# Copying the sample's and the cross units' probabilities by DMA into fp32r tiles before they are transposed

## The chip, the cores and the metric

The kernel runs on one core of one Trainium2 chip. The metric is the device time of one execution in microseconds; a time given for a kernel is the median of several runs, and a profile is one further execution with the hardware profiler on. Five engines work in parallel, each through its own list in order: TensorE (PE; its weight loads are shown apart as PEld), VectorE (DVE), ScalarE (ACT), GpSimd (POOL) and SyncE (SP), which here only issues DMAs. ACT's queue issues DMAs too.

## The reference

One layer of an encoder for two inputs with the same weights, a prompt of 1024 tokens and a sample of 512, both with 1024 channels and 256 memory tokens. Cut to what matters:

```python
h = rms_norm(x, ln_pre)
z = h @ w_in                      # q, k, v, gates, cross queries, merge logits
pool_out  = multiscale_pool(pool_in, w_pool, pool_scale)
attn_out  = softmax(q @ k.T * scale) @ v            # 8 heads of 64, 2 kv heads
cross_out = softmax(xq @ mk.T * scale) @ mv         # 4 heads of 128, 256 memory tokens
merged = sum(sigmoid(merge_n) * ((branch_n * silu(gate_n)) @ w_branch[n]) for n in range(3))
y = x + rms_norm(merged @ w_out, ln_post)
```

All of it is in float32. The kernel multiplies in fp32r, a reading of float32 that PE takes at a higher rate; each operand is split into a high and a low part (`split`: ACT copies into an fp32r tile, DVE subtracts), and three or two products of the parts are added up.

## The kernel before

Weights come in tiles of 128x1024 (`raw`), are split into `whi` and `wlo`, and are used once. First all projections of the prompt are made, then those of the sample. The softmax work is cut into **units**, which `stream` (line 918) walks through as a pipeline. There are 64 attention units of the prompt (128 queries, 1024 keys), 8 cross units of the prompt, 16 pair units of the sample's attention (`pairs_of`, two blocks of 128 queries by 512 keys), and 4 cross units of the sample (`cross`, 512 queries by 256 memory tokens, one head each), in that order. The text calls the last four c0 to c3.

Step i of `stream` calls, for several units at once: `ahead` two units early (loads), `scores` of unit i (matmuls into a PSUM tile `A`, then row maximum on DVE, exponentials on ACT into an SBUF tile `u`, reciprocal on DVE, normalization on POOL in place), `turn` of unit i-3 (eight transposes of 128x128 on PE into another `A`, then `split` into a `med` tile), `values` of unit i-6 (matmuls with v), and `hand` of unit i-1. `weave` fills the rest of PE's time from another stream of work: the sample's projections and, near the end of the units, the first merge phase of `branches` (matmuls written B<-med,whi and B<-med,wlo).

The normalized probabilities are plain f32, since POOL writes them. For the 64 attention units, `hand` (line 810) copies them by a DMA on ACT's queue (line 814) into a second `u` tile of type fp32r, and `turn` transposes that with the identity `identr`. The pair and the cross units have no `hand` (None in their tuples): `turn` transposes the f32 tile with `ident`, and the tile is held until then.

There are 7 buffers for `u`, 14 for `med`, 9 for `hu`, 3 for `A`, 2 for `B`. The order on each engine is not the order of the code: a scheduler sets it when the program is built, by priorities (`tc.high_priority`) and by its own idea of durations, and it also decides which buffer a tile takes. So a change of one operation moves others.

Of the kernel before, what the change touches and what calls it, by code (L numbers as in the profile page):

```python
# [12 lines left out]
F32 = mybir.dt.float32  # L13
F32R = mybir.dt.float32r
# [5 lines left out]
P = 128  # L20
D = 1024
KC = D // P
BLK = 512
TT = BLK // P
NH, NG, HD = 8, 2, 64
NXH, XHD, NMEM = 4, 128, 256
# [36 lines left out]
def encoder_kernel(ctx: ExitStack, tc, wt, xs, xts, mt, cols, rows, rope, edge, ys):  # L63
    nc = tc.nc
    v, act, pool, pe = nc.vector, nc.scalar, nc.gpsimd, nc.tensor
# [10 lines left out]
    def nm(s):  # L76
        count[0] += 1
        return f"{s}_{count[0]}"

    def U(dt=F32, n=D):  # L80
        return sb.tile([P, D + 2 * PAD], dt, tag="u", bufs=NU, name=nm("u"))[:, :n]

    def M(dt=F32R):
        return sb.tile([P, 2048], dt, tag="med", bufs=NM, name=nm("med"))
# [7 lines left out]
    def A(dt=F32):  # L92
        return ps.tile([P, 1024], dt, tag="A", bufs=3, name=nm("A"))
# [32 lines left out]
    def mm(out, l, r, **k):  # L126
        cost[0] += out.free_size() / 2.4
        pe.matmul(out, l, r, **k)  # L128

    def tr(out, x, i):  # L130
        cost[0] += 107 if i is ident else 56
        pe.transpose(out, x, i[:])  # L132
# [7 lines left out]
    def load(out, src):  # L140
        return nc.sync.dma_start(out, src)  # L141
# [3 lines left out]
    ident = const.tile([P, P], F32, name="ident")  # L145
    make_identity(nc, ident)
    identr = const.tile([P, P], F32R, name="identr")
# [15 lines left out]
    def lo_of(out, x, hi):  # L163
        v.tensor_tensor(out, x, hi.bitcast(F32), op=ALU.subtract)  # L164

    def split(hi, lo, x):
        act.activation(hi, x, AF.Copy)  # L167
        lo_of(lo, x, hi)
# [599 lines left out]
    def from_scratch(field, bs, dt=F32):  # L768
# [3 lines left out]
            load(t[:, c * BLK:(c + 1) * BLK], field[c][:, bs])  # L772
        return t

    def attention(b, sc, kt, vt):

        bs = slice(b * BLK, (b + 1) * BLK)
        qd, gd, out = sc["q"], sc["attn_gate"], sc["br1"]
        nch = KC
        units = [(jp, hd, j) for jp in range(TT // 2) for hd in range(NH) for j in range(2)]  # L780
        state = {}

        def ahead(i):
            jp, hd, j = units[i]
            for k, x in ((3, 0), (1, 1)):
                if i == 0 or (i + k) % (2 * NH) == 0 and i + k < len(units):
                    at = 0 if i == 0 else jp + 1
                    if x == 0:
                        state["q", at] = M()
                    load(state["q", at][:, x * D:(x + 1) * D].bitcast(F32), qd[b * TT + at * 2 + x][:])  # L790

        def scores(i):
            jp, hd, j = units[i]
            g = hd // (NH // NG)
            q = state["q", jp][:, j * D + hd * P:j * D + (hd + 1) * P]
            a = A()
            for n in range(2):
                ns = slice(n * 512, n * 512 + 512)
                mm(a[:, ns], q, kt[g][0][:, ns], start=True, stop=False)
                mm(a[:, ns], q, kt[g][1][:, ns], start=False, stop=True)  # L800
            mx, sm, rc = S(1), S(1), S(1)
            with tc.high_priority(PMAX):
                v.reduce_max(mx[:], a[:], axis=AX.X, negate=True)  # L803
                p = U()
                act.activation(p, a[:], AF.Exp, bias=mx[:], accum_out=sm[:])  # L805
            v.reciprocal(rc[:], sm[:])  # L806
            pool.tensor_scalar(p, p, rc[:], 1.0, op0=ALU.mult, op1=ALU.mult)  # L807
            state[i] = p

        def hand(i):  # L810

            p = state[i]
            state[i] = U(F32R)
            act.dma_start(state[i].bitcast(F32), p)

        def turn(i):
            jp, hd, j = units[i]
            p = state.pop(i)
            if j == 0:
                state["pt", i // 2] = M()[:], M()[:]  # L820
            pv = [t.rearrange("p (c j n) -> p c j n", c=nch, j=2) for t in state["pt", i // 2]]
            tp = A(F32R)
            for c in range(nch):
                tr(tp[:, c * P:(c + 1) * P], p[:, c * P:(c + 1) * P], identr)
            tv = tp[:].bitcast(F32).rearrange("p (c n) -> p c n", c=nch)
            with tc.high_priority(PTURN):
                split(pv[0][:, :, j], pv[1][:, :, j], tv)

        def values(i):

            jp, hd, j = units[i]
            g = hd // (NH // NG)
            if j == 0:
                state["o"] = B()
            o, pts = state["o"], state["pt", i // 2]
            for c in range(j * nch // 2, (j + 1) * nch // 2):
                for s in range(2):
                    mm(o[:, :256], vt[:, c, g].rearrange("p s d -> p (s d)"), pts[s][:, c * 256:(c + 1) * 256],
                       start=(c == 0 and s == 0), stop=(c == nch - 1 and s == 1))
            if j == 0:  # L840
                return
            del state["pt", i // 2]
            gated(state, jp, hd, o, gd, out, b)

        return [(ahead, scores, turn, values, hand, i, 2560) for i in range(len(units))]

    def pairs_of(sc, kt, vt):

        qd, gd, out = sc["q"], sc["attn_gate"], sc["br1"]
        units = [(jp, hd) for jp in range(TT // 2) for hd in range(NH)]  # L850
        state = {}

        def ahead(i):
            jp, hd = units[i]
            for k, x in ((2, 0), (1, 1)):
                if i == 0 or (i + k) % NH == 0 and i + k < len(units):
                    at = 0 if i == 0 else jp + 1
                    if x == 0:
                        state["q", at] = M()
                    load(state["q", at][:, x * D:(x + 1) * D].bitcast(F32), qd[at * 2 + x][:])  # L860

        def scores(i):
            jp, hd = units[i]
            g = hd // (NH // NG)
            a, p = A(), U()
            mx, sm, rc = S(2), S(2), S(2)
            for j in range(2):
                q, ns = state["q", jp][:, j * D + hd * P:j * D + (hd + 1) * P], slice(j * BLK, (j + 1) * BLK)
                mm(a[:, ns], q, kt[g][0], start=True, stop=False)
                mm(a[:, ns], q, kt[g][1], start=False, stop=True)  # L870
            with tc.high_priority(PMAX):
                v.reduce_max(mx[:], a[:].rearrange("p (j n) -> p j n", j=2), axis=AX.X, negate=True)
                for j in range(2):
                    ns = slice(j * BLK, (j + 1) * BLK)
                    act.activation(p[:, ns], a[:, ns], AF.Exp, bias=mx[:, j:j + 1], accum_out=sm[:, j:j + 1])
            v.reciprocal(rc[:], sm[:])
            for j in range(2):
                ns = slice(j * BLK, (j + 1) * BLK)
                pool.tensor_scalar(p[:, ns], p[:, ns], rc[:, j:j + 1], 1.0, op0=ALU.mult, op1=ALU.mult)
            state[i] = p  # L880

        def turn(i):
            p, tp, pt = state[i], A(), M()
            for c in range(4):
                for j in range(2):
                    tr(tp[:, c * 256 + j * P:c * 256 + (j + 1) * P], p[:, j * BLK + c * P:j * BLK + (c + 1) * P], ident)
            with tc.high_priority(PTURN):
                split(pt[:, :D], pt[:, D:], tp[:])
            state[i] = pt

        def values(i):
            jp, hd = units[i]
            o, pt = B(), state.pop(i)
            for c in range(4):
                for s in range(2):
                    mm(o[:, :256], vt[:, c, hd // (NH // NG)].rearrange("p s d -> p (s d)"),
                       pt[:, s * D + c * 256:s * D + (c + 1) * 256], start=(c == 0 and s == 0), stop=(c == 3 and s == 1))
            gated(state, jp, hd, o, gd, out, 0)

        return [(ahead, scores, turn, values, None, i, 2560) for i in range(len(units))]  # L900

    def gated(state, jp, hd, o, gd, out, b):
        r = slice((hd % 2) * 64, (hd % 2) * 64 + 64)
# [31 lines left out]
    def cross(b, sc, mkd, mvd, mem):  # L935
# [3 lines left out]
        state = {}  # L939
# [36 lines left out]

        def turn(c):
            p = state[c]
            tp = A()
            for m in range(2):  # L980
                for t in range(TT):
                    tr(tp[:, m * 512 + t * P:m * 512 + (t + 1) * P], p[:, t * 256 + m * P:t * 256 + (m + 1) * P], ident)
            pt = M()
            split(pt[:, 0:1024], pt[:, 1024:2048], tp[:])
            state[c] = pt

        def values(c):
# [8 lines left out]
                v.tensor_tensor(g[:], o[:], g[:], op=ALU.mult)  # L996
            finished.append((out[c][:, bs], g[:]))

        return [(ahead, scores, turn, values, None, c, 3410) for c in range(NXH)]

    def branches(b, sc, merged):

# [171 lines left out]
    units = [u for b in range(2) for u in attention(b, sc, kt, vt)]  # L1174
# [109 lines left out]
```

## Time and profile before

| | us |
|---|---|
| median of 3 runs | 1461.84 (1461.23 to 1462.43) |
| the profiled execution | 1459.46 |
| its span, first to last instruction | 1457.6 |
| PE busy | 1430.3 |
| DVE busy | 966.1 |
| ACT busy | 711.4 |
| POOL busy | 280.3 |

Lines of the form "L132 PE MATMUL A<-identr,u" name the source line, the engine, the operation and the tiles; L128 is the helper for all matmuls, L132 that for all transposes, L141 that for loads, L164 and L167 the two halves of a split. L814 is the copy in `hand`, L803 to L807 the softmax of the attention units, L872 to L879 that of the pair units, L966 to L974 that of the cross units, L996 the gate behind a cross unit's values, L1061 the evacuation of a merge. Something like [2.3 <-DVE med L1061] says how long the engine was idle ahead of the row and what released it. In the windows view each row is a stretch with the busy time of each engine in it.

### The profile page before, as it was taken

The numbers are of one execution on the slowest core, as the hardware profiler recorded it, in microseconds if no ns is written. First come the engines' busy times: TensorE is split into PE (matmuls) and PEld (weight loads), VectorE is DVE, ScalarE is ACT, GpSimd is POOL, SyncE is SP. The second block draws the span as 40 slices with busy tenths as digits, with TensorE's granted clock in tenths as the row PEclk, the third lists the DMA queues.
The fourth block names the chain that finished last, engine by engine and source line by source line (L and its number), as shares of the span: only waits on it lengthen the run. The fifth ranks groups of instructions, "written<-read, shape, count | busy, mean of one in ns | idle before, by whom it ended". The sixth has DMA issues, their size and how long they took to land. (4 is left out here: it accounts for less than half of the span.)

```text
span 1457.6 us, 19545 instructions
## 1 busy us (share of the span) xinstructions
PE 1430.3 (98%) x7264; PEld 1197.1 (82%) x7264; DVE 966.1 (66%) x1211; ACT 711.4 (49%) x1085; POOL 280.3 (19%) x286
## 2 busy tenths in 40 slices
PE   7999999999999999999999999999999999999998
PEld 5878888888888888788888888888888788888887
DVE  6896585766547664665777666686776665665654
ACT  6454444454434544443666666676676223323322
POOL 1000010110000000210223332233342230240241
PEclk9999999999999999999999999999999999999999
DMA  8312243332331444244655665565357834954942
GB/s 292 122 58 95 79 145 104 120 123 68 125 101 62 154 143 133 84 158 163 244 187 193 216 238 192 186 223 184 127 181 244 278 119 157 332 189 157 333 156 82
DMA packets 95375, 238.65 MB, mean 164 GB/s; under 512 B 10672, under 2 KB 18992, under 8 KB 95280
## 3 DMA queue, kind: packets, MB, share of 16 engines
q1 hardware_dynamic: 86064, 203.84, 42.2%
q10 hardware_dynamic: 9216, 33.56, 5.9%
q8 instruction: 57, 0.93, 0.3%
q14 instruction: 38, 0.31, 0.1%
HBM read 151.38 MB, written 52.43 MB: 140 GB/s over the span
## 5 line engine op out<-in xcount | busy, mean ns | idle before, releaser
L128 PE MATMUL B<-med,whi 128*128 128x512 f32 x1576 | 492.4, 393 | 4.5 <-DVE med L1061 2.3
L128 PE MATMUL A<-med,whi 128*128 128x512 f32 x1200 | 373.9, 392 | 1.4 <-ACT med L167 1.0
L128 PEld LDWEIGHTS B<-med,whi 128*128 128x128 f32 x1576 | 291.4, 188 | 64.5 <-DVE med L1061 2.7
L128 PE MATMUL B<-med,wlo 128*128 128x512 f32 x788 | 308.3, 391 | 0.5 <-DVE wlo L164 0.5
L167 ACT ACTIVATE whi<-raw 128x1024 fp32r<-128x1024 f32 (+1 forms) x169 | 167.3, 990 | 283.7 <-PE A L128 147.9
L164 DVE TENSOR_TENSOR wlo<-raw,whi 128x1024 fp32r<-128x1024 f32 (+1 forms) x169 | 210.0, 1243 | 138.1 <-ACT whi L167 137.6
L128 PEld LDWEIGHTS A<-med,whi 128*128 128x128 f32 x1200 | 223.0, 188 | 48.3 <-ACT med L167 1.2
L128 PE MATMUL A<-med,wlo 128*128 128x512 f32 x600 | 234.1, 390 | 0.1
L128 PEld LDWEIGHTS B<-med,wlo 128*128 128x128 f32 x788 | 147.9, 188 | 32.4 <-DVE wlo L164 1.3
L189 POOL TENSOR_SCALAR s<-s 128x16 f32<-128x16 f32 (+3 forms) x17 | 7.5, 444 | 660.9 <-DVE s L582 324.0
L128 PEld LDWEIGHTS A<-med,wlo 128*128 128x128 f32 x600 | 112.6, 188 | 24.7 <-DVE wlo L164 1.0
L164 DVE TENSOR_TENSOR med<-A,med 128x1024 fp32r<-128x1024 f32 (+1 forms) x93 | 112.8, 1214 | 28.4 <-ACT med L167 26.7
L167 ACT ACTIVATE med<-A 128x1024 fp32r<-128x1024 f32 x92 | 94.2, 1025 | 68.8 <-PE A L132 68.4
L807 POOL TENSOR_SCALAR u<-u,s 128x1024 f32<-128x1024 f32 x64 | 72.1, 1126 | 211.8 <-DVE s L806 174.6
L1063 POOL TENSOR_TENSOR med<-med,hu 128x512 f32<-128x512 f32 x48 | 78.7, 1650 | 130.2 <-DVE hu L1061 130.2
L803 DVE TENSOR_REDUCE s<-A 128x1 f32<-128x1024 f32 x64 | 77.8, 1215 | 37.0 <-PE A L128 33.8
L128 PE MATMUL A<-whi,med 128*128 128x512 f32 (+1 forms) x352 | 98.3, 360 | 0.0
L805 ACT ACTIVATE u<-A,s 128x1024 f32<-128x1024 f32 x64 | 71.3, 1114 | 40.6 <-issue 23.4
L128 PE MATMUL A<-kt,med 128*128 128x512 f32 x320 | 87.7, 395 | 0.0
L167 ACT ACTIVATE whi<-sum 128x1024 fp32r<-128x1024 f32 x50 | 52.9, 1061 | 60.3 <-PE B L128 36.5
L164 DVE TENSOR_TENSOR med<-med,med 128x1024 fp32r<-128x1024 f32 (+1 forms) x50 | 55.2, 1115 | 37.8 <-ACT med L167 34.0
L167 ACT ACTIVATE med<-med 128x1024 fp32r<-128x1024 f32 (+1 forms) x44 | 44.3, 1018 | 69.6 <-POOL med L1063 41.7
(199 smaller groups left out, 1915.3 us busy)
## 6 DMA issues: line engine op xcount, KB each, us to landing
raw<-wt SPq DMA_DIRECT2D x168, 512.0 KB, 3.7
u<-u ACTq DMA_DIRECT2D x64, 512.0 KB, 3.2
merge<-hu SPq DMA_DIRECT2D x72, 256.0 KB, 2.2
hu<-merge SPq DMA_DIRECT2D x72, 256.0 KB, 5.3
med<-br SPq DMA_DIRECT2D x36, 256.0 KB, 5.3
q<-hu SPq DMA_DIRECT2D x24, 256.0 KB, 2.5
br<-hu SPq DMA_DIRECT2D x24, 256.0 KB, 2.7
med<-q SPq DMA_DIRECT2D x12, 512.0 KB, 4.8
```

The source lines that it names most:

```text
L128: pe.matmul(out, l, r, **k)
L164: v.tensor_tensor(out, x, hi.bitcast(F32), op=ALU.subtract)
L167: act.activation(hi, x, AF.Copy)
L189: pool.tensor_scalar(ss, ss, EPS, 1.0, op0=ALU.add, op1=ALU.mult)
L803: v.reduce_max(mx[:], a[:], axis=AX.X, negate=True)
L805: act.activation(p, a[:], AF.Exp, bias=mx[:], accum_out=sm[:])
L807: pool.tensor_scalar(p, p, rc[:], 1.0, op0=ALU.mult, op1=ALU.mult)
L1063: pool.tensor_tensor(at, at, sg[:], op=ALU.add)
```

## The change

`hand` moves out of `attention` into a helper `hand_on(state)`, and the pair and cross units pass it too. Their `turn` then reads the fp32r copy, with `identr` and a PSUM tile of type fp32r, whose bits are read as f32 for the split.

```diff
+    def hand_on(state):
+        def hand(i):
+
+            p = state[i]
+            state[i] = U(F32R)
+            act.dma_start(state[i].bitcast(F32), p)
+        return hand
...
-        return [(ahead, scores, turn, values, hand, i, 2560) for i in range(len(units))]
+        return [(ahead, scores, turn, values, hand_on(state), i, 2560) for i in range(len(units))]
...
-            p, tp, pt = state[i], A(), M()
+            p, tp, pt = state[i], A(F32R), M()
...
-                    tr(tp[:, c * 256 + j * P:c * 256 + (j + 1) * P], p[:, j * BLK + c * P:j * BLK + (c + 1) * P], ident)
+                    tr(tp[:, c * 256 + j * P:c * 256 + (j + 1) * P], p[:, j * BLK + c * P:j * BLK + (c + 1) * P], identr)
             with tc.high_priority(PTURN):
-                split(pt[:, :D], pt[:, D:], tp[:])
+                split(pt[:, :D], pt[:, D:], tp[:].bitcast(F32))
...
-        return [(ahead, scores, turn, values, None, i, 2560) for i in range(len(units))]
+        return [(ahead, scores, turn, values, hand_on(state), i, 2560) for i in range(len(units))]
...
-            tp = A()
+            tp = A(F32R)
...
-                    tr(tp[:, m * 512 + t * P:m * 512 + (t + 1) * P], p[:, t * 256 + m * P:t * 256 + (m + 1) * P], ident)
+                    tr(tp[:, m * 512 + t * P:m * 512 + (t + 1) * P], p[:, t * 256 + m * P:t * 256 + (m + 1) * P], identr)
...
-            split(pt[:, 0:1024], pt[:, 1024:2048], tp[:])
+            split(pt[:, 0:1024], pt[:, 1024:2048], tp[:].bitcast(F32))
...
-        return [(ahead, scores, turn, values, None, c, 3410) for c in range(NXH)]
+        return [(ahead, scores, turn, values, hand_on(state), c, 3410) for c in range(NXH)]
```

The orders show two places at the end of the stream. On PE before, the transposes of c1, c2 and c3 (A_10184, A_10253, A_10300) at the point where the first merge matmul (B_10212) begins:

```order
L128 MATMUL B_10125<-med_4471,wlo_10122 128x512
L132 MATMUL A_10184<-ident,u_9988 128x128 x8
L132 MATMUL A_10253<-ident,u_10058 128x128 x8
L132 MATMUL A_10300<-ident,u_10109 128x128 x8
L128 MATMUL B_10212<-med_10196,whi_10208 128x512
L128 MATMUL B_10225<-med_10069,med_4528 128x256 x8
```

The same place in the change, where A_10192 is c0, A_10238 is c1, A_10309 is c2, and B_10266 the first merge matmul:

```order
L132 MATMUL A_10192<-identr,u_10088 128x128 x8
L128 MATMUL B_10177<-med_4468,whi_10173 128x512
L128 MATMUL B_10177<-med_4468,wlo_10174 128x512
L128 MATMUL B_10177<-med_4471,whi_10173 128x512 x2
L128 MATMUL B_10177<-med_4471,wlo_10174 128x512
L128 MATMUL B_10177<-med_4471,whi_10173 128x512 x2
L128 MATMUL B_10177<-med_4471,wlo_10174 128x512
L132 MATMUL A_10238<-identr,u_10142 128x128 x8
L132 MATMUL A_10309<-identr,u_10218 128x128
L128 MATMUL B_10266<-med_10250,whi_10262 128x512
L128 MATMUL B_10279<-med_10119,med_4528 128x256 x5
```

Before, three units were transposed in a row ahead of the merge; now c0 and c1 are, with the first of c2's eight transposes, while the other seven of c2 and all of c3's stand further back among the merge matmuls. Between c3's scores (A_10144, not shown) and c2's first transpose stand 13 matmuls of 512 columns, 8 of values and these 16 transposes.

On ACT in the change, from the copy of c1 to the split of c1 (the copies are of c1, u_10142, and of c2, u_10218; the exponentials are c3's):

```order
L780 DMA u_10142<-u_10036 128x1024
L505 ACTIVATE hu_10233<-B_10177,hbias 128x512
L972 ACTIVATE u_10161,s_10158<-A_10144,s_10157 128x256 x4
L167 ACTIVATE whi_10338<-raw_10336 128x1024
L167 ACTIVATE med_10201<-A_10192 128x1024
L780 DMA u_10218<-u_10108 128x1024
L167 ACTIVATE med_10247<-A_10238 128x1024
```

The copy of c2, on which c2's transposes wait, stands behind c3's exponentials, a split of weights and the split of c0. Before, no DMA stood in this part of ACT's list. Line numbers in the change: the copy is L780, `attention`'s softmax 8 lines lower down than before, and everything from `pairs_of` on 2 lines lower down (L970 becomes L972).

More of the change, by code (lines that the diff above doesn't have):

```diff
@@ L808, in scores @@
             state[i] = p
[L810 to L814, printed above, removed]
         def turn(i):
```

## The prediction

> **What bounds the kernel now.** I read the page first: the busy shares, the slices and the clock.
>
> ```profile
> span 1457.6 us, 19545 instructions
> PE 1430.3 (98%) x7264; PEld 1197.1 (82%) x7264; DVE 966.1 (66%) x1211; ACT 711.4 (49%) x1085; POOL 280.3 (19%) x286
> PEclk9999999999999999999999999999999999999999
> ```
>
> TensorE (PE) is busy for 98% of the span. Matmul ends are modelled, so that share alone proves little; the stretches say where PE has no gap at all. Columns: the stretch in us and its length, busy time of PE, weight loads, DVE, ACT and POOL, then granted clock, DMA share and GB/s. The units that the change touches run from about 978 to 1112.
>
> ```profile
> 978.00:1085.00 107.00, 107.00 (x634) 92.36 (x633) 76.62 (x98) 73.78 (x164) 40.76 (x63) 1.00 0.49 160
> 1085.00:1112.00 27.00, 26.20 (x181) 23.93 (x180) 20.74 (x26) 22.62 (x54) 12.59 (x20) 1.00 0.64 212
> 1144.00:1300.00 156.00, 155.75 (x688) 128.61 (x687) 99.11 (x100) 49.10 (x59) 52.02 (x36) 1.00 0.63 214
> ```
>
> PE is full in the first stretch, short of 0.8 us in the second, and after 1144 short of 0.25 us in 156. So in this kernel PE time is the time: what PE saves before 1112 brings the end forward, and what PE waits there is not given back later. The second stretch is also the one in which ACT is nearly full: 22.62 of 27 us, 84%, against 69% before it. That matters, because the change puts its new work on ACT.
>
> **The transposes, part by part.** 28 units (16 pairs, 12 cross units) with 8 transposes each change from f32 to fp32r, 224 in all. First eight of the kind that is wanted (identr), then eight of the kind that is there (ident), each with what stands behind it on PE; columns are start and duration.
>
> ```profile
> 965.01 0.79 PE L132 MATMUL A<-identr,u 128*128 128x128 f32 x8
> 965.64 1.17 PE L128 MATMUL B<-med,vt 128*128 128x256 f32 x8
> 966.65 1.60 PE L128 MATMUL A<-med,u 128*128 128x256 f32 x12
> 979.75 1.03 PE L132 MATMUL A<-ident,u 128*128 128x128 f32 x8
> 980.54 1.19 PE L128 MATMUL B<-med,vt 128*128 128x256 f32 x8
> 981.57 0.63 PE L128 MATMUL B<-med,whi 128*128 128x512 f32 x2
> 968.32 0.80 PE L132 MATMUL A<-identr,u 128*128 128x128 f32 x8
> 968.95 0.47 PE L128 MATMUL B<-med,whi 128*128 128x512 f32 x1
> 969.25 0.39 PE L128 MATMUL B<-med,wlo 128*128 128x512 f32 x1
> 1022.79 0.39 PE L128 MATMUL B<-med,whi 128*128 128x512 f32 x1
> 1023.09 1.07 PE L132 MATMUL A<-ident,u 128*128 128x128 f32 x8
> 1023.91 0.47 PE L128 MATMUL B<-med,whi 128*128 128x512 f32 x1
> 1024.23 0.40 PE L128 MATMUL B<-med,wlo 128*128 128x512 f32 x1
> ```
>
> From the start of the transposes to the start of the piece after the next: 1.64 us for fp32r (965.01 to 966.65), 1.82 for f32 (979.75 to 981.57): 0.18 less for a unit. Behind a 512-wide matmul the f32 kind costs more: 1022.79 to 1024.23 is 1.44 with the matmul ahead of it, whose own pitch is 0.23, so 1.21, against 0.93 for fp32r (968.32 to 969.25): 0.28 less. In the chain of waits the f32 groups last 0.87 us as a rule, and 0.95 or more in five of the 28, where the dear case is. The first and the last of these five:
>
> ```profile
> 1023.18 0.98 PE A L132 x8
> ...
> 1080.64 0.95 PE A L132 x8
> ```
>
> 23 x 0.18 + 5 x 0.28 = **5.5 us less on PE**. Bounds: 28 x 0.16 (the starts alone, 0.79 against 0.63) = 4.5, and 28 x 0.28 = 7.8.
>
> The Trainium skill speaks of this in "FP8 and Floating Point Precision", section "TensorE Precision Notes": true fp32 makes four passes through the array, the reduced reading one. By that rule the eight f32 transposes would take four times the 0.63 us and the change would save some 53 us, an estimate. The rows above disagree, with 0.79 against 0.63, and the rows decide.
>
> **What is added: 28 copies on ACT's queue.** Each is one issue, with this row, and it moves 512 KB between two tiles:
>
> ```profile
> L814 ACTq DMA_DIRECT2D u<-u x64: 472/472/507, 689.4 to 967.8; - x64
> DMA to landing us min/median/max: 2.9/3.2/6.8
> q10 hardware_dynamic: 9216, 33.56, 5.9%
> PE A L132 <- DMA u<-u: 0.2, 1, 0.2
> ```
>
> An issue holds ACT for 0.47 us, 28 of them 13 us over 134 us: ACT goes from 69% to about 79% in the first stretch, and to 92% in the second if five fall there. The DMA engines: 5.9% of 1457.6 us for 64 copies is 1.34 us each, so 28 add 0.28 of share to 0.49 and 0.64. Both fit; I put the bandwidth at nothing, and at up to 1 us if the weight loads that hide behind PE come late.
>
> In the steady part the latency is covered. By the change's own orders a copy is issued right behind the exponentials of the next unit, and its transposes stand at least 7.8 us of PE work (at the pitches above) behind that unit's scores; the attention units have the same distance, and the last row shows what PE lost to their 64 copies: 0.2 us, once. The pair units need somewhat more of it than attention, since they have two exponentials. I cost them at nothing, at most 2 us. The u tiles: a probability is now held for about one step and its copy for two, one tile of the seven more at a time. The order cannot say what that costs; ACT's exponentials would wait for a buffer, and the same 2 us bounds it. No copy goes through SP's or POOL's queue. ACT's issue waits for POOL's normalization of the unit before, which by the order of ACT is a whole unit old, except at the end.
>
> **The end of the stream** is where the cover is thin. The last four units are the sample's cross units, c0 to c3. Before, PE did the transposes of c1, c2 and c3 in one block of 24 at 1108.42, half a us after the last probability was ready. In the change (the orders shown in the section on the change) the first transpose of c2 stands close behind c3's scores, and c2's copy stands on ACT behind c3's four exponentials, one split of weights and the split of c0. Rows of before for these pieces:
>
> ```profile
> 1099.67 1.59 PE L128 MATMUL A<-med,u 128*128 128x256 f32 x12
> 1103.84 0.47 ACT L970 ACTIVATE u<-A,s 128x256 f32<-128x256 f32 x1 [1.43 <-DVE s L966]
> 1105.65 1.04 ACT L167 ACTIVATE med<-A 128x1024 fp32r<-128x1024 f32 x1
> 1108.39 1.06 ACT L167 ACTIVATE whi<-raw 128x1024 fp32r<-128x1024 f32 x1 [1.30 <-PE B L128]
> L966 DVE TENSOR_REDUCE s<-A 128x4 f32<-128x1024 f32 x9 | 10.9, 1212 | 0.8 <-POOL u L974 0.8
> 1098.89 0.95 PE B L128 x8
> 1101.26 2.75 PE B L128 x12
> 1108.42 2.78 PE L132 MATMUL A<-ident,u 128*128 128x128 f32 x24
> 1112.08 0.50 PE L128 MATMUL B<-med,whi 128*128 128x512 f32 x1 [0.87 <-ACT med L167]
> ```
>
> PE, from the end of c3's scores to c2's first transpose in the new order: 13 matmuls of 512 columns (2.75 / 12 = 0.229 each, 2.98 us), eight values (0.95) and the 16 transposes of c0 and c1 (0.70 for eight): **5.3 us**. ACT, from the same moment: before, c3's scores ended at 1101.26 and its exponentials began at 1103.84, 2.58 us later. Four take 1.81 (1103.84 to 1105.65), then 1.06 for the weights, 1.04 for the split of c0, and 3.2 until the copy lands: **9.7 us**. The difference, **4.4 us**, PE stands still, since it takes its work in order and 12 matmuls of the next phase and everything behind them queue behind that transpose. Bounds: if the exponentials begin as soon as a reduction of 1.21 us allows (1.3 us behind the scores) and the copy lands in 2.9, the wait is 2.8; if the copy takes the longest time seen, 6.8, it is 8.0. I take the middle, since in the new order c0's and c1's scores stand next to each other on PE, so ACT can hardly have less of a backlog than it had at 1103.84. What goes away is the wait of 0.87 us at 1112.08 for ACT's split: by the time the copy has landed that split is done.
>
> A wait of this length also touches the clock. What the profile shows of that is at the kernel's start, a matmul that waited and the three stretches around it (PE alone: length, busy, clock, DMA):
>
> ```profile
> 25.70 0.55 PE L128 MATMUL A<-mh,whi 128*128 128x512 f32 x1 [2.84 <-ACT whi L167]
> 24.00:28.00 4.00, 2.01 (x5) 0.75 0.75 267
> 28.00:32.00 4.00, 4.00 (x17) 0.82 0.71 257
> 32.00:36.00 4.00, 4.00 (x25) 1.00 0.14 47
> 1143.33 0.73 PE L128 MATMUL B<-med,whi 128*128 128x512 f32 x2 [2.29 <-DVE med L1061]
> ```
>
> After 2.84 us without work the granted clock was 0.75 and 0.82 for 8 us, (0.25 + 0.18) x 4 = **1.7 us** lost; after 2.29 us at 1143 nothing was (1.00 in the stretch from 1144). So a wait of 4.4 us costs 1.7 on top, one below about 2.8 nothing. The Trainium skill has this in "TensorE: Matmul & The Clock Gate", section "Part 1: The HAM clock gate (the "warmup" mystery)": a window of about 3.4 us without matmuls halves the clock until a busy one has passed. By that rule the price would be half a window, 1.7 us, an estimate; the row agrees in size and shows it for a shorter gap.
>
> The wait of 2.29 us at 1143 hangs on loads that SP issues between the stores of c1 and c2. In the new order fewer gate loads stand ahead of them but one evacuation less ahead of their split on DVE: I leave it, with -2.3 to +1.
>
> **Sum**, against the profiled execution's span of 1457.6 us (its run 1459.46, the median of the runs 1461.84, some 2.4 above it; the difference is carried over unchanged): -5.5 + 4.4 - 0.9 + 1.7 = **-0.3 us**, so 1461.5.
>
> **Rivals.** *The end of the stream is covered.* For it: PE arrives later or ACT earlier than I think, the wait stays under 2.8 us, and the clock holds: -5.5 + 2.8 - 0.9 = -3.6, 1458.2; with no wait at all -6.4, 1455.4. Against it: ACT's durations leave 8.1 us of the 9.7 even at their best (1.3 + 1.81 + 2.1 + 2.9), and PE has 5.3. *The copies land late.* At the end of the stream the DMA share is 0.64 and the copies add 0.28; a copy of 6.8 us has been seen among the 64. From a landing of 6.4 us on the tail costs more than the transposes save by what can be told: with 6.8 the wait is 8.0, the sum -5.5 + 8.0 - 0.9 + 1.7 = +3.3, 1465.1. For it speaks the load there, against it the median of 3.2 over 64 copies. *The transposes get no cheaper*, if their weight loads and not the matmuls set the pace: then +5.2, 1467.0; the pitch of 0.63 against 0.79 in one kernel speaks against it. *The clock's rule alone with a shorter wait*: a gap between 2.8 and 4.4 that still drops the clock gives -1.9, 1459.9, on the side of my forecast.
>
> **How the numbers follow.** What a measurement of this kernel can tell is about 0.2%, 2.9 us. Gain and wait cancel to within that: 0.52. Covered tail: 0.28. Late copies: 0.16, transposes no cheaper: 0.04. So faster 0.28, within 0.52, slower 0.20. The time predicted is that of the likeliest, 1461.5, whose own range is 1459.0 to 1464.5. The whole range takes in half of the covered tail below (5.5 saved with little wait, 1456.5) and the late copies above, 1465.5.
>
> **What would show it.** In the profile of the changed kernel: f32 transposes by ident only outside the units, and eight by identr from about 978 on with 0.63 between starts; 92 copies on ACT's queue; one PE wait of 3 to 6 us near 1110 released by a DMA u<-u, with the granted clock under 1 in the 4 us behind it; the wait of 0.87 gone; PE full between 978 and 1100. I am wrong if no such wait is there, if waits for copies or buffers are spread over the pair units, or if the store and load waits around 1140 grow by several us.

## The result, and the profile after

The change is slower: 1473.66 us as the median of 4 runs (1470.88 to 1476.28) against 1462.13 for the kernel before (1461.23 to 1464.95). The ratio is 1.0071, with a 95% interval of 1.0056 to 1.0087, so 8 to 13 us. The prediction was 1461.5, about the time of the kernel before, with a range of 1456.5 to 1465.5; the change lies 8 us above its upper end. The profiled execution of the change took 1474.33 us, its span 1472.5.

The page of the changed kernel, in the lines that answer to those shown of before:

```profile
span 1472.5 us, 19574 instructions
PE 1433.3 (97%) x7264; PEld 1196.8 (81%) x7264; DVE 964.6 (66%) x1211; ACT 711.3 (48%) x1085; POOL 279.8 (19%) x286
PEclk9999999999999999999999999999998999999999
q10 hardware_dynamic: 13248, 48.24, 8.4%
u<-u ACTq DMA_DIRECT2D x92, 512.0 KB, 3.3
```

The 92 copies are there, their median landing is as before (among the copies issued from 980 on it is 4.1 us), and PE's busy share hardly moved. Only one slice of the clock shows that something went wrong. The loss has to be looked for by stretch. The same stretches of 20 us, first before, then after (length, busy PE, weight loads, DVE, ACT, POOL, then clock, DMA share, GB/s):

```profile
1000.00:1020.00 20.00, 20.00 (x109) 16.89 (x108) 13.22 (x18) 11.47 (x30) 6.41 (x12) 1.00 0.53 168
1020.00:1040.00 20.00, 20.00 (x110) 16.48 (x109) 14.33 (x18) 11.95 (x24) 5.81 (x8) 1.00 0.54 174
1040.00:1060.00 20.00, 20.00 (x123) 17.35 (x123) 14.26 (x19) 15.22 (x30) 7.56 (x11) 1.00 0.26 81
1100.00:1120.00 20.00, 19.13 (x112) 16.45 (x111) 13.94 (x17) 13.53 (x28) 5.16 (x10) 1.00 0.83 272
1120.00:1140.00 20.00, 20.00 (x90) 16.54 (x89) 11.10 (x13) 4.02 (x4) 0.00 (x0) 1.00 0.88 285
```

```profile
1000.00:1020.00 20.00, 18.81 (x114) 15.86 (x113) 12.85 (x16) 12.25 (x28) 6.93 (x14) 1.00 0.87 311
1020.00:1040.00 20.00, 18.23 (x92) 14.57 (x91) 14.18 (x18) 11.10 (x22) 4.11 (x6) 0.98 0.90 311
1040.00:1060.00 20.00, 20.00 (x118) 17.07 (x118) 13.12 (x18) 12.63 (x25) 7.25 (x9) 0.93 0.48 177
1100.00:1120.00 20.00, 15.59 (x107) 13.60 (x105) 13.48 (x19) 16.36 (x43) 9.19 (x16) 0.94 0.65 219
1120.00:1140.00 20.00, 15.77 (x74) 13.20 (x75) 10.72 (x13) 5.47 (x7) 1.24 (x3) 0.80 0.89 329
```

There are two places. In the middle, 1000 to 1060, PE was full before and now misses 3.0 us, while the DMA share of 1000 to 1040 rose from 0.53 to about 0.9 and the clock sagged behind it. At the end of the stream, 1100 to 1140, PE misses 8.6 us and the clock is down to 0.80. The four large waits of PE in the timeline, with what released each in brackets:

```profile
1011.31 0.74 PE L128 MATMUL A<-kt,med 128*128 128x512 f32 x2 [1.19 <-DMA med<-q]
1038.70 0.75 PE L128 MATMUL B<-med,whi 128*128 128x512 f32 x2 [1.77 <-DVE hu L998]
1116.82 0.84 PE L132 MATMUL A<-identr,u 128*128 128x128 f32 x8 [2.06 <-DMA u<-u]
1124.05 0.34 PE L132 MATMUL A<-identr,u 128*128 128x128 f32 x1 [6.39 <-DMA u<-u]
```

The last two are c1's and c2's transposes, 8.45 us together. The first two do not wait for a copy at all: one waits for a load of q, the other for DVE, which itself waited for a load of a cross unit's gate. That is seen on DVE:

```profile
1037.96 0.69 DVE L998 TENSOR_TENSOR hu<-B,hu 128x512 f32<-128x512 f32 x1 [1.58 <-DMA hu<-x_gate]
```

Not all of the difference between the two profiled executions is the change. The first unit that the change touches starts its transposes 4.8 us later than before (the first row below; before, 979.75), though nothing ahead of it was changed. A run without any new copy, which stands among the experiments as e3_poolr, is 3.9 us later at that point (second row):

```profile
984.53 0.80 PE L132 MATMUL A<-identr,u 128*128 128x128 f32 x8
```

```profile
983.61 0.80 PE L132 MATMUL A<-identr,u 128*128 128x128 f32 x8
```

In the other profiled executions of kernels that are the same up to there, at a mean clock of 0.99 or more, this point lies between 980.44 (e1_pairs) and 984.25 (e1_cross), so it varies by some 4 us whatever the change. So 14.9 us of span are 4.8 us ahead of the changed units, which vary from execution to execution, and 10.1 us from them on, close to the 8 to 13 of the timed runs.

### The profile page after: what moved, and what is told of

It is laid out like the page before. It is cut to its first block, busy times and chain, and to the rows that moved or that the text cites. A ratio compares the mean times of both kernels' runs of the same rounds, so it can differ in the third digit from the quotient of the medians.

```text
span 1472.5 us, 19574 instructions
## 1 busy us (share of the span) xinstructions
PE 1433.3 (97%) x7264; PEld 1196.8 (81%) x7264; DVE 964.6 (66%) x1211; ACT 711.3 (48%) x1085; POOL 279.8 (19%) x286
## 5 line engine op out<-in xcount | busy, mean ns | idle before, releaser
L132 PEld LDWEIGHTS A<-identr,u 128*128 128x128 f32 x736 | 72.2, 140 | 24.1 <-issue 8.9
L132 PE MATMUL A<-identr,u 128*128 128x128 f32 x736 | 74.4, 244 | 10.6 <-DMA u<-u 10.1
L167 ACT ACTIVATE whi<-sum 128x1024 fp32r<-128x1024 f32 x50 | 52.9, 1060 | 60.2 <-PE B L128 35.5
```

## The experiments

Theory A: the loss sits at the end of the stream, where c1's and c2's transposes wait for copies that land late, with nothing else for PE to do. Theory B: the load of 28 copies on the DMA engines makes other loads late, in the middle of the stream above all. The runs say that both are true and about equal, and that the gain is smaller than was worked out. Each ratio is to the kernel before, timed together with the run (1461.6 to 1463.8).

| run | median us | ratio (95%) |
|---|---|---|
| the change | 1473.66 | 1.0071 (1.0056 to 1.0087) |
| e1_not_last4 | 1468.87 | 1.0037 (1.0022 to 1.0052) |
| e1_pairs | 1469.40 | 1.0040 (1.0025 to 1.0054) |
| e1_cross | 1466.65 | 1.0032 (1.0018 to 1.0047) |
| e2_f32_copy | 1476.77 | 1.0088 (1.0073 to 1.0102) |
| e3_poolr | 1461.56 | 0.9994 (0.9982 to 1.0005) |
| e4_idle_copies | 1468.05 | 1.0035 (1.0022 to 1.0048) |
| e5_before_noload | 1463.35 | 1.0006 (0.9996 to 1.0016) |
| e5_after_noload | 1486.47 | 1.0124 (1.0080 to 1.0168) |
| e8_after_noload | 1474.63 | 1.0083 (1.0063 to 1.0103) |
| e6_before_share60 | 1465.06 | 1.0014 (1.0003 to 1.0026) |
| e6_after_share60 | 1468.35 | 1.0035 (1.0021 to 1.0049) |
| e6_poolr_share60 | 1461.52 | 0.9992 (0.9978 to 1.0006) |
| e6_after_gates | 1468.21 | 1.0033 (1.0020 to 1.0045) |
| e7_idle_gates | 1466.87 | 1.0024 (1.0015 to 1.0034) |
| e7_after_gates_share62 | 1467.67 | 1.0026 (1.0011 to 1.0040) |
| e7_poolr_all | 1460.31 | 0.9979 (0.9969 to 0.9989) |
| e7_poolr_all_60 | 1457.07 | 0.9958 (0.9943 to 0.9973) |
| e9_poolr_all_60_gates | 1453.42 | 0.9930 (0.9913 to 0.9946) |

### Which units cost

The edit is the same in kind each time: the hand-over is taken out of some of the 28 units, and their transposes go back to float32.

```diff
-        return [(ahead, scores, turn, values, hand_on(state), c, 3410) for c in range(NXH)]
+        return [(ahead, scores, turn, values, None, c, 3410) for c in range(NXH)]
```

> Copies for the 8 prompt cross units and the 16 pair units; the last four units (sample cross c0 to c3) are transposed in float32 as before. If the loss is only the wait for the last copies with no work left behind it (8.45 us of waits and the clock drop at 1116 to 1128 in the trace of the change), the gain of 24 x 0.22 = 5.3 us stays and this kernel is faster than before: 1456 to 1459. If the copies' load on the DMA engines costs as much in the middle of the stream (3.2 us of waits and 1.8 us of clock between 1000 and 1060 in that trace), it lands near the kernel before: 1460 to 1464. If every copy costs about the same (11.5 + 6 over 28 copies, 0.62 us each, less 0.22), it stays slow: 1470 to 1473.

> Copies for the 16 pair units alone; all 12 cross units are transposed in float32 as before. Tail alone: 1461.8 - 16 x 0.22 = 1458. Load in the middle counts too: the trace of the change loses about 5 us to late loads and the clock around the pair units, so 1461 to 1465. Every copy costs 0.4 us net: 1468.

> Copies for the 12 cross units alone (8 of the prompt, before the pairs, and the last 4). Tail alone: the waits of 8.45 us and 4 us of clock at the end stay, less 0.9 us for the wait of before and 12 x 0.22 = 2.6 us: 1469 to 1472, so most of the loss with 12 of 28 copies. Every copy costs 0.4 us net: 1466 to 1467.

Without the last four copies 1468.87 remains, with the 16 pairs alone 1469.40, with the 12 cross units alone 1466.65. Each group loses, so neither "the tail alone" (1458 for the pairs) nor "every copy the same" (1470 to 1473 without the last four) holds throughout, though e1_cross alone came out where the second put it (1466 to 1467). The last four copies make 1.0071 - 1.0037 = 0.0034 of the loss, some 5 us; the 16 pairs make the other 5 or 6 and the 8 cross units of the prompt about none, within these intervals. The pairs' loss is not a wait for their copies: in e1_pairs PE's largest wait between 980 and 1112 is again the gating line, and behind it the clock is halved (timeline, then the stretches around it):

```profile
1035.26 1.22 PE L128 MATMUL B<-med,whi 128*128 128x512 f32 x2 [2.86 <-DVE hu L998]
```

```profile
1032.00:1036.00 4.00, 1.14 (x4) 0.64 (x3) 1.48 (x2) 0.42 (x2) 0.00 (x0) 0.82 1.03 373
1036.00:1040.00 4.00, 4.00 (x11) 3.13 (x10) 2.29 (x5) 1.45 (x4) 1.36 (x2) 0.50 0.57 206
```

### The copies without the gain, the load without the wait, the gain without the copies

e2_f32_copy makes the copies but transposes them in float32:

```diff
-            state[i] = U(F32R)
-            act.dma_start(state[i].bitcast(F32), p)
+            state[i] = U()
+            act.dma_start(state[i], p)
```

> All 28 new copies are made, but into float32 tiles, and transposed in float32: the copies without the cheaper transposes. If the transposes' gain is on the path (0.22 us in each of 28 units), this kernel is 5 to 6 us slower than the change: 1478 to 1480. If the end waits for the copies' landing and swallows what PE gained in the last units, the difference is under 5: 1475 to 1478. If transposes were never on the path: the same as the change, 1473.7.

e4_idle_copies is the kernel before with copies that no one reads:

```diff
+    def hand_idle(state):
+        def hand(i):
+            act.dma_start(U(), state[i])
+        return hand
```

> The kernel before, and beside it the 28 copies, which nobody reads: the transposes still take the float32 tile at the old time. This is the load on the DMA engines alone. If the middle waits (loads of q and of the gates that land late) come from the load, they stay: 1465 to 1469, with the same waits on the gating line near 1036 and on q near 1010, and no wait on a copy. If what costs is that the transposes wait for their own copies, this kernel is the same as the kernel before: 1461 to 1463.

e3_poolr has the cheaper transposes and no new copy:

```diff
-                pool.tensor_scalar(p[:, ns], p[:, ns], rc[:, j:j + 1], 1.0, op0=ALU.mult, op1=ALU.mult)
-            state[i] = p
+                pool.tensor_scalar(pr[:, ns], p[:, ns], rc[:, j:j + 1], 1.0, op0=ALU.mult, op1=ALU.mult)
+            state[i] = pr
```

> No new copies: in the 28 units POOL's scaling writes its product straight into an fp32r tile, which the transposes then read; so the probabilities are rounded to fp32r there. This is the cheaper transposes alone, with the same number of tiles as the change. If a transposing group is really 0.22 us cheaper on the path, 28 x 0.22 = 6 us are won: 1455 to 1457. If the loss comes from the other allocation of tiles and not from the copies, the middle waits are there without them and it lands at 1463 to 1468.

The three take the change apart. The copies that no one reads cost 0.0035 (1468.05, some 5 us). Making the transposes depend on the copies adds 0.0088 - 0.0035 = 0.0053, some 8 us. The cheaper transposes take 0.0088 - 0.0071 = 0.0017 back, 2 to 3 us; with intervals of 0.0015 to either side of both ratios, this last difference is not clear of nothing. In e4 PE's waits in the middle are on the gating line, as theory B said, and on no copy (none on q either, which was expected as well); the loads of q and of the gates that were issued between 985 and 1005 landed in 4.1 and 3.4 us before (first fence) and in 5.3 and 7.2 in e4 (second; its line of the gate multiply is L1002):

```profile
med<-q SPq DMA_DIRECT2D x2, 512.0 KB, 4.1
hu<-x_gate SPq DMA_DIRECT2D x3, 256.0 KB, 3.4
```

```profile
med<-q SPq DMA_DIRECT2D x2, 512.0 KB, 5.3
hu<-x_gate SPq DMA_DIRECT2D x3, 256.0 KB, 7.2
```

```profile
1010.19 1.65 PE L128 MATMUL B<-med,med 128*128 128x512 f32 x6 [1.01 <-DVE hu L1002]
1038.62 0.74 PE L128 MATMUL B<-med,whi 128*128 128x512 f32 x2 [1.48 <-DVE hu L1002]
```

The Trainium skill says in "DMA: Bandwidth & Descriptors", section "Issuing engines are not separate DMA queues", that transfers issued from different engines end up on the same 16 DMA engines and interleave; these rows agree: the copies are issued from ACT, and it is SP's loads that land late.

e3_poolr missed its expectation of 1455 to 1457: 1461.56, within 0.2% of before. Its middle is clean, so a second tile for each unit costs nothing by itself; it is not held for as long as in the change, though. Up to c0's transposes the gain is there: from the first changed unit to c0 PE took 1104.01 - 983.61 = 120.40 us, before 1103.85 - 979.75 = 124.10, so 3.7 us in 24 units, 0.154 each. At the end of the stream it is partly given back:

```profile
1104.01 0.80 PE L132 MATMUL A<-identr,u 128*128 128x128 f32 x8
1108.43 2.38 PE L132 MATMUL A<-identr,u 128*128 128x128 f32 x24
1112.54 0.50 PE L128 MATMUL B<-med,whi 128*128 128x512 f32 x1 [1.73 <-ACT med L167]
```

```profile
1112.00:1116.00 4.00, 3.26 (x13) 2.70 (x14) 3.69 (x4) 3.38 (x5) 0.20 (x1) 0.77 0.84 279
1116.00:1120.00 4.00, 4.00 (x16) 3.19 (x15) 1.42 (x2) 0.37 (x1) 0.53 (x1) 0.80 0.72 235
```

PE comes earlier to the point where it waits for ACT's split: 1.73 us in place of 0.87, and behind that the clock is 0.77 and 0.80 for 8 us, 1.7 us more.

### The loads around the end

```diff
-                    load(x, src[t * P:(t + 1) * P, :])
+                    if not bare_end:
+                        load(x, src[t * P:(t + 1) * P, :])
```

> The change without the load of the post-norm weights and the four loads of x in the first block's out phase (2.6 MB that are fetched around the end of the stream; the output lacks that weight and the residual there). If these loads make the last copies land in 5 to 7 us instead of 3.3, the two waits shrink from 8.45 to about 3 us and the clock drop goes with them: 1464 to 1467. If the last copies are late because they are issued late in ACT's order, little is won: 1471 to 1473.

> The kernel before without the same loads: the yardstick for the run above. Its wait of 2.29 us near 1143 for a gate load goes if these loads delay it: 1459 to 1460; otherwise 1462.

> The change without the loads of the post-norm weights and of x in the first block's out phase, once more, since the earlier run of it was disturbed. If those 2.6 MB make the last copies land late: 1464 to 1467, with the waits on the copies of c1 and c2 at 3 us or less together. If the gate and weight loads of the same stretch, or the order, do it: 1471 to 1474, with 6 us or more before c2's first transpose.

In its profiled execution e5_after_noload had a mean granted clock of 0.927, where the change had 0.991, so its time can't be compared; e8 repeats it. Leaving the loads out does not help: 1474.63, against 1463.35 for the kernel before without the same loads. The waits on the copies of c1 and c2 are nearly those of the change, 7.7 us together:

```profile
1114.40 0.85 PE L132 MATMUL A<-identr,u 128*128 128x128 f32 x8 [1.11 <-DMA u<-u]
1121.83 0.34 PE L132 MATMUL A<-identr,u 128*128 128x128 f32 x1 [6.57 <-DMA u<-u]
```

So these 2.6 MB are not what makes the last copies late. The trace of the change shows what had the DMA engines instead. c2's copy was issued at 1116.97; in the stretch 1117 to 1121 the queue of the copies (q10) moved 0.02 MB, and that of the loads (q1) held 74% of the engines (packets, MB, share):

```profile
q1 hardware_dynamic: 420, 0.77, 74.4%
q10 hardware_dynamic: 6, 0.02, 1.5%
```

The copy's 512 KB went between 1121 and 1124. The loads that the change issued between 1112 and 1120 are two of weights of 512 KB, five merge gates and one x_gate of 256 KB; no run took them away.

### More work behind the last units, and earlier gate loads

The share of fill that is woven into each unit is lowered, so that more is left for the end:

```diff
-LAG, VLAG, SHARE, LOOK, WAIT = 3, 2, 0.66, 1, 6
+LAG, VLAG, SHARE, LOOK, WAIT = 3, 2, 0.60, 1, 6
```

> The change, with SHARE 0.60 for 0.66: less fill is woven into each unit, so that the stream's last units have more; in PE's order there stand then 10 rows of other work or more between the transposes of any two of the last four units, where the change has c2's first transpose right behind c1's. If the end costs because PE has nothing between these transposes while the copies are under way, the waits of 2.06 and 6.39 us shrink to 0 to 3 together and the clock drop (about 4 us) goes: 1463 to 1467. If the copies' landing delays everything in any order, it stays at 1471 to 1474.

> The kernel before with SHARE 0.60: the yardstick for the run above. Its waits at the end are 0.87 and 2.29 us: 1460 to 1463 if only these move, up to 1466 if the stream's middle misses the fill.

> No new copies, the probabilities written as fp32r by POOL, and SHARE 0.60. With SHARE 0.66 the cheaper transposes alone won 0.9 us where 28 x 0.22 = 6 was worked out. If PE's gain was given back at the end of the stream (its wait on an evacuation went from 0.87 to 1.73 us, and the clock fell to 0.91 over 20 us), more fill there keeps it: 4 to 6 us below the yardstick of this call. If a transpose is no cheaper on the path, it equals the yardstick.

The gate's load moves from a cross unit's values to its transposes:

```diff
         def turn(c):
             p = state[c]
+            g = state["g", c] = HU()
+            load(g[:], gd[c][:, bs])
...
-            g = HU()
-            load(g[:], gd[c][:, bs])
+            g = state.pop(("g", c))
```

> The change, with the cross units' gate loads (x_gate) issued at the unit's transposes, two steps earlier than at its values, and nothing else. If the wait near 1038 (1.77 us, on the gating line, with about 1.8 us of clock) comes from that load landing late under the copies' load, it goes: 1469 to 1471. If something else holds that multiply, it stays: 1473 to 1474.

Both helped. With SHARE 0.60 the change takes 1468.35, a little above what theory A said, on a yardstick that is itself 2 us up: the distance to it is 0.0021 in place of 0.0071; the large waits at the end of the stream are gone and the clock holds (e6_after_share60):

```profile
1100.00:1120.00 20.00, 19.04 (x107) 15.51 (x106) 11.08 (x14) 13.38 (x27) 5.46 (x9) 1.00 0.75 258
1120.00:1140.00 20.00, 20.00 (x88) 16.05 (x87) 10.48 (x13) 4.99 (x6) 0.00 (x0) 1.00 0.94 318
```

With the earlier gate loads it takes 1468.21, below what was expected; the middle has no wait on the gating line, one of 0.7 us on a copy, and the clock is full there in spite of a DMA share of 0.81 to 1.00 (e6_after_gates):

```profile
1000.00:1020.00 20.00, 19.19 (x104) 15.63 (x103) 14.68 (x18) 13.01 (x31) 5.63 (x11) 1.00 1.00 357
1020.00:1040.00 20.00, 20.00 (x117) 16.82 (x116) 14.35 (x18) 11.59 (x23) 5.68 (x10) 1.00 0.81 285
```

So in the middle busy DMA engines as such cost little; a load that is issued just in time and comes late does. At the end this kernel still waits, 2.91 us for c1's copy and 3.42 ahead of c2's first transpose, 6.3 us together where the change has 8.45. e6_poolr_share60 came out 0.0022 below its yardstick, 3.5 us where 4 to 6 were expected.

> The 28 copies that nobody reads, as in the earlier run (1468.05), with the cross units' gate loads issued two steps earlier. If the copies' load costs time by making those loads land late, the waits on the gating line (1.0 near 1010 and 1.5 near 1038) go: 1465 to 1466. If other loads are late as well (weights, merge gates at the end), most of the 5 us stays: 1467 to 1468.

> The change with both cures: the gate loads two steps earlier, and SHARE 0.62, so that other work stands between the last units' transposes. Each alone took 5.3 to 5.5 us off the change. If they cure two different waits, they add: 1462 to 1464, the time of the kernel before. If both took away the same clock drop and wait, together they give no more than one: 1467 to 1469.

With idle copies the earlier gates take the ratio from 1.0035 to 1.0024, between the two expectations and too little to decide; where the rest of the load's price lies was not found, since the profiled execution of e7_idle_gates had a mean granted clock of 0.65 and can't be read against the others. The two cures together do not add: 1467.67, no better than each alone. The waits have moved again, the largest of them to a copy of the prompt's attention, at a place that was quiet before:

```profile
731.10 1.23 PE L132 MATMUL A<-identr,u 128*128 128x128 f32 x8 [3.56 <-DMA u<-u]
```

With less fill in each unit a copy's landing is no longer covered in the steady part either. In these runs what was saved at one end was missing at the other as long as a copy stood between softmax and transpose.

### No copies at all

That POOL writes the probabilities does not oblige them to be plain f32: in e3_poolr it wrote the fp32r tile itself. Here the prompt's attention, too, gets its fp32r tile from POOL:

```diff
-            pool.tensor_scalar(p, p, rc[:], 1.0, op0=ALU.mult, op1=ALU.mult)
-            state[i] = p
+            pool.tensor_scalar(pr, p, rc[:], 1.0, op0=ALU.mult, op1=ALU.mult)
+            state[i] = pr
```

> No copies at all, in the 64 units of the prompt's attention either: POOL writes the scaled probabilities as fp32r (rounded) in all 92 units. If the waits on copies in the prompt's units (0.58, 0.47 and 0.20 us in the run without new copies) are the copies' alone: 1459.5 to 1461, one or two us below the 1461.6 of that run. If the same transposes wait for POOL instead: 1461 to 1462.

> The same with SHARE 0.60, where the prompt's units waited 4.6 us for copies (0.59, 2.45 and 1.53) and the end waited little. If those waits go with the copies: 1456 to 1458, faster than both kernels. If a unit with less fill then waits for its own scaling instead: 1460 to 1462.

> No copies (POOL writes fp32r in all 92 units), SHARE 0.60, and the cross units' gate loads two steps earlier. In the run without the last of these one wait is left at the end of the stream: 2.58 us on the gating line, with the clock at 0.68 and 0.89 in the 8 us behind it (1.7 us). If that gate load is late for want of an early issue, both go: 1453 to 1455. If the gates need their buffers or the DMA engines are full there (share 0.86), it stays or another load takes its place: 1456 to 1458.

All three came out inside what was expected: 1460.31, 1457.07 and 1453.42. The second had one large wait left, on the gating line, and the third, which issues that load earlier, has none. PE's largest wait between 690 and 1160, first in e7_poolr_all_60, then in e9_poolr_all_60_gates:

```profile
PE B L128 <- DVE hu L998: 2.6, 1, 2.6
```

```profile
PE B L128 <- DVE hu L490: 0.5, 2, 0.3
```

At 0.9930 (0.9913 to 0.9946) it beats both kernels, by 10 us and by 20. It need not be the same computation to the last bit: the copy by DMA takes a probability over as it is, while POOL writes its product in the type fp32r; no run measured the difference in the output. How much of the 10 us the kernel before would gain from the earlier gates alone was not run; with SHARE 0.60 alone it lost 2 us.

## Why the prediction was wrong, point by point

**The gain, -5.5.** The mechanism was right: 0.63 us between starts for eight, as predicted. The size was not: 0.154 us per unit in e3_poolr, about the lower bound of 0.16, so 28 x 0.154 = 4.3. The step that failed is "what PE saves before 1112 brings the end forward". PE was full, but at 1112 it met a wait whose end ACT sets, and there part of the saved time became waiting (0.86 us more) and a clock drop (1.7 us): net 0.9 us (2.6 gained to 0.7 lost, by the interval) in e3_poolr. It became a gain only when the end had other work: with SHARE 0.60 and without copies 3.5 us below the yardstick.

**The steady part, "I cost them at nothing, at most 2 us", and the bandwidth "at up to 1 us".** This is the first large miss: about 5 us from copies that no one reads (3 to 7 by the interval of e4_idle_copies). The failing step is that a share of 0.28 added to 0.49, an average over 107 us, was taken to fit. The average came out nearly so (0.72 over 980 to 1100, 0.50 before), but in 1000 to 1040 the share was 0.87 to 0.90. Of the loads issued between 985 and 1005, those of q landed in 7.4 us in place of 4.1 and those of gates in 5.9 in place of 3.4, and the gate loads were issued just ahead of their use. The prediction considered what waits for copies, and the weights; what had no slack was a third party: a load of q, and loads of the gate for which DVE waited, with PE behind it.

The wait at 1038 has a second cause. Its gate load was hardly slower than before (5.2 us to landing, where the two in that place took 4.8 and 5.0) but was issued late, behind a store that waited for ACT:

```profile
1032.38 0.32 SPq L506 DMA_DIRECT2D merge<-hu  x1
1032.76 2.20 SPq L141 DMA_DIRECT2D hu<-x_gate  x2
```

In e4 the same load went out ahead of that store, at 1030.28, and took 7.6 us. An earlier issue helps against both, so e6_after_gates does not part them.

What the prediction said of ACT, 0.47 us held by each issue, is not borne out either: c2's issue runs from 1116.97 to 1117.44, and the split behind it begins at 1117.18 (rows below). One of the prediction's signs of being wrong, "waits for copies or buffers" spread over the pair units, comes near to what happened; the waits were there, but for loads.

**The wait at the end, +4.4.** Measured 2.06 + 6.39 = 8.45, at the place named and with the releaser named; the rival of late copies had 8.0. PE's work between c3's scores and c2's first transpose is 1124.05 - 1110.08 (c3's scores end 1.67 behind 1108.41) - 8.45 = 5.5, as predicted (5.3). ACT's chain is 14.0 us in place of 9.7. The pieces, on PE and on ACT in the change:

```profile
1108.41 1.67 PE L128 MATMUL A<-med,u 128*128 128x256 f32 x12
1114.79 0.69 ACT L505 ACTIVATE hu<-B,hbias 128x512 f32<-128x512 f32 x1 [1.15 <-PE B L128]
1115.38 0.47 ACT L972 ACTIVATE u<-A,s 128x256 f32<-128x256 f32 x1
1116.97 0.47 ACTq L780 DMA_DIRECT2D u<-u  x1
1117.18 1.07 ACT L167 ACTIVATE whi<-raw 128x1024 fp32r<-128x1024 f32 x1
1118.12 1.95 ACT L167 ACTIVATE med<-A 128x1024 fp32r<-128x1024 f32 x2
```

The exponentials begin 5.3 us behind the scores (1115.38), not 2.58: ahead of them ACT did those of c2 (1111.71 to 1113.6), then waited 1.15 us for PE's own fill and evacuated it. The copy is issued 1.6 us later, during the exponentials and ahead of the two splits that I had counted with 2.1 us. And PE starts 7.1 us behind the issue (1116.97 to 1124.05; the copy lands after 6.9), where 3.2 was counted. So +2.7, -2.3 and +3.9 against the prediction's pieces. That the first two nearly cancel is luck, and so is how close the rival's 8.0 came. The landing is the mis-sized term; the prediction took the median over 64 copies from a stretch with a DMA share of 0.59 for one with about 0.9.

**The clock, +1.7.** The size of one drop was right: in 1120 to 1128 PE worked 3.95 us at a clock of 0.50, 2.0 us lost. But there was a second drop in the middle, 0.02 and 0.07 of 20 us, 1.8 us; and the bound "below about 2.8 nothing" fell, as the last section shows.

```profile
1120.00:1128.00 8.00, 3.95 (x13) 3.40 (x14) 4.22 (x4) 1.97 (x3) 0.49 (x2) 0.50 1.00 388
```

**The wait of 0.87, -0.9, and the one of 2.29, left alone with -2.3 to +1.** Both went; 1.5 us in three pieces came in their place, perhaps since the loads catch up while PE stands, which no run shows (PE's waits in the change: us in total, times, longest):

```profile
PE B L128 <- DVE med L1063: 1.5, 3, 0.7
```

Summed again with the measured terms, from the first changed unit on: -4.3 + 8.45 (end) + 2.0 (clock there) + 3.2 + 1.8 (middle: waits of 1.19, 1.77 and 0.2, and the clock) - 0.9 - 2.3 + 1.5 = +9.5, against 10.1 in the two traces.

## What to carry to other kernels

Before a stretch gets more DMA traffic, ask which loads in it are issued just in time, and by whom they are waited for: in the middle of this stream it was these that came late, and PE waited for none of the added transfers there. Take the share and the landing time from the very stretch, not from an average over it or a median over another one. And time saved on an engine that is full reaches the end only if no wait set by another engine lies behind it; moving some filler work to that wait, or taking the transfer out of the chain, was worth more here than the faster instruction.

## What the runs showed of the hardware that was not expected

The clock falls after shorter waits than the prediction's 2.84 us, and not after each. The wait of 1.77 us in the change ended at 1038.70; the clock was 0.82 in the stretch around that moment and 0.50 in the next (first fence), though PE was at work again, and 0.77 and 0.80 after the 1.73 us in e3_poolr. After 2.29 us in the kernel before it stayed at 1.00 (second fence):

```profile
1038.00:1040.00 2.00, 1.30 (x4) 1.11 (x5) 2.00 (x3) 0.00 (x0) 0.00 (x0) 0.82 1.00 361
1040.00:1042.00 2.00, 2.00 (x6) 1.52 (x6) 1.57 (x3) 0.34 (x1) 1.37 (x2) 0.50 0.96 366
```

```profile
1143.00:1147.00 4.00, 3.67 (x16) 3.06 (x17) 2.83 (x4) 2.01 (x2) 0.00 (x0) 1.00 0.89 293
```

The Trainium skill, "TensorE: Matmul & The Clock Gate", section "Part 1: The HAM clock gate (the "warmup" mystery)", has a free-running window of about 3.4 us, and the half clock after an idle one. That the outcome differs from place to place would fit a free-running window; that 1.7 us of idleness is enough does not fit, and the measurement decides.

In the change a DMA's issue on ACT's queue did not stand behind the activations ahead of it as another activation would: c2's copy, listed behind a split of weights and a split of c0, was issued at 1116.97, and these began at 1117.18 and 1118.12.
